# A first attention pair multiplied in plain fp32 instead of split products, and the order of work around it

## The chip, the cores and the metric

The kernel runs on one core of a Trainium2 chip. The metric is the device time of one execution in microseconds (us); the median of several executions is compared. The engines that matter are TensorE (PE, matrix products), VectorE (DVE), ScalarE (ACT), GpSimd (POOL) and SyncE (SP, whose queue issues the transfers).

## What is computed

One layer of a streaming encoder for 512 prompt tokens and 32 sample tokens, T = 544 tokens together, model width 2048. The input x is normalised, multiplied by one wide weight `w_in`, and the result goes to three groups of heads: eight retention heads, four spatial-gating groups, four heads of cross-attention to a memory of 256 tokens. The gated outputs are multiplied by `w_out` and added to x. All data are float32. The part that matters here:

```python
h = rmsnorm(x, g_norm)
proj = h @ w_in                            # 2048 -> 6656 columns
kv = rmsnorm(mem, g_mem) @ w_mem_kv        # keys and values of the memory
mk, mv = jnp.split(kv, 2, axis=-1)
...
sc = jnp.einsum('blhd,bmhd->bhlm', aq, mem_k) * (XA_HEAD_DIM ** -0.5)
p = jax.nn.softmax(sc, axis=-1)
ao = jnp.einsum('blhm,bmhd->blhd', p, mem_v) * silu(ag)
...
out = x + jnp.concatenate([ro, go, ao], axis=-1) @ w_out
```

## The kernel before

**Products in split form.** A float32 operand is split into a rounded high part (`copy`, ACT, line 87) and the rest as low part (`tt` with subtract, DVE, line 90); each product of a block is three matmuls: high x high, high x low, low x high (`multiply`, line 222). Plain float32 matmuls are used for small things only, such as scores (`sc`), transposes (`pT_ps`) and `ao`; in the profile each of these shows as two records.

**Pairs and blocks.** The columns of `w_in` are handled in pairs of 128 columns, called xa0 to xa3 (query and gate of an attention head), then qk and vg for the retention heads, gv and gg, and eight output pairs o0 to o7. In a pair the activations, laid out by feature, are cut in a 2 x 2 grid: two halves of the features (the outer index of `xk`) and two halves of the tokens (272 each). The blocks of x are called h11 and h21 (first feature half, first and second tokens), h12 and h22 (second feature half). Their split forms live in `A["11"]`, `A["21"]`, `A["12"]`, `A["22"]`.

**Seven products instead of eight.** All pairs but the first ones (xa0, o0) use seven block products on sums of blocks (`project`, line 238). For these the kernel makes S1 = h21 + h22, S2 = S1 - h11, S3 = h11 - h21 and S4 = h12 - S2 and splits each. Likewise sums of weight blocks are made (`sources`, line 173: t2, t1, t3, t4). The first pair xa0 uses the plain eight block products (`plain`, line 324), while the sums are made in `between` on the side.

**Weights ahead.** `begin` (line 198) loads a pair's two weight halves, forms the next block's weight sum and copies its high part; `ahead` (line 209) takes the low part of the oldest begun block and begins the next. `product` calls `ahead` and then multiplies. High and low weight parts have three buffers each, raw weight halves three ("raw").

**The start.** In the order written: the keys of the memory (`kps`, steps `key_unit`), the values (`value_unit` splits a weight chunk, `value` multiplies it into `vps`), and meanwhile the row sums for the two norms: `square_mem` and `halve` give rm for the memory, `square_x` (ACT, with a running sum) gives r for x. `token_factors` takes the power -0.5 on POOL, `diagonals` and `to_all_partitions` spread the factors over the partitions through PE; the results are `rm_bc` and `r_bc`. `scale_x` multiplies x by the gain and r (DVE, line 93), `split_x` and `block` split it. Then come xa0, xa1 (with the first head of `attend`) and so on. `attend` is a generator; `project` takes one step of it after each product: sigmoid part of the gate, scores and softmax, empty steps, transposes, output.

**Order.** `put` (line 82) keeps an instruction in program order on its engine as long as `fixed[0]` is true; it becomes false at the end of xa0. After that the framework orders the instructions itself. Transfers are issued on SP in the order of the loads: memory and key weights, tokens (`xt`, x by tokens for the row sums), value weights (`wv`), x by features (`x`, four quarters of 1088 KB), weights of xa0 (`wxa`).

Of the kernel before, what the change touches and what calls it, by code (L numbers as in the profile page):

```python
# [14 lines left out]
P = 128  # L15
# [8 lines left out]
XH = 4  # L24
# [52 lines left out]
def step_kernel(ctx: ExitStack, tc: tile.TileContext, a, o):  # L77
# [88 lines left out]
    def load_half(i, half):  # L166
        if i < len(ORDER):
            w = W.setdefault(ORDER[i], {})
            if half not in w:
                w[half] = raw_weight(f"w{ORDER[i]}_{half}")  # L170
                nc.sync.dma_start(out=w[half].rearrange("p k b c -> p (k b c)"), in_=a["w"][i, half])
# [21 lines left out]
    FOUR = {"xa0": ("11", "12", "21", "22"), "o0": ("11", "12", "21", "22"),  # L193
# [15 lines left out]
    def ahead(more=True):  # L209

        if done[0] < len(units):
            if done[0] == len(begun):
                begin()
            name, key = units[done[0]]
            src, u = begun[done[0]]
            tt(u[1], src, u[0].bitcast(F32), ALU.subtract)
            W[name][key] = u
            done[0] += 1
            if more:
                begin()  # L220
# [60 lines left out]
    def silu2(x, th):  # L281

        nc.scalar.activation(out=th, in_=x, func=AF.Tanh, scale=0.5)
        stt(x, th, 1.0, x, ALU.add, ALU.mult)
# [53 lines left out]
    with tc.tile_pool(name="mkv", bufs=1, reuse_waits="tile") as mkv, ExitStack() as ctx_x:  # L338
# [3 lines left out]
        with tc.tile_pool(name="pa", bufs=1, reuse_waits="tile") as pa:  # L342
# [31 lines left out]
            def halve(x, k):  # L374
                while k > 1:
                    k //= 2
                    tt(x[:, 0:k], x[:, 0:k], x[:, k:2 * k], ALU.add)
                return x[:, 0]
# [45 lines left out]
            load_tokens(3)  # L424
            load_x(0, 4)
            wv.append(load_kv("wv", 2))
# [11 lines left out]
            def square_mem(u):  # L438
                i, ks = u // 4, slice(u % 4 * 2, u % 4 * 2 + 2)
                put(nc.scalar.activation(out=mem[i][:, ks], in_=mem[i][:, ks], func=AF.Square))  # L440

            def key_unit(u):
                i, k0 = u // 4, u % 4 * 2
                if u < 8:
                    w, src = unit(f"k{u}", [P, 2, 512]), wk[u // 2][:, u % 2 * 2:u % 2 * 2 + 2]
                    if u:
                        copy(w[0], src)
                    for k in (k0, k0 + 1):
                        copy(mm[i][0][:, k], mem[i][:, k], scale=gm[:, KS * i + k:KS * i + k + 1])
                    if not u:  # L450
                        copy(w[0], src)
                    tt(w[1], src, w[0].bitcast(F32), ALU.subtract)
                    for k in (k0, k0 + 1):
                        stt(mm[i][1][:, k], mem[i][:, k], gm[:, KS * i + k:KS * i + k + 1], mm[i][0][:, k].bitcast(F32),
                            ALU.mult, ALU.subtract)
                    ku[u] = w
                if u:
                    square_mem(u - 1)
# [9 lines left out]
            for u in range(8):  # L468
                key_unit(u + 1)
                if u == 4:  # L470
                    part0 = halve(mem[0], KS)
                elif u == 6:
                    value_unit(0)
                    square_x(0)
                elif u == 7:
                    value_unit(1)
                    part1 = halve(mem[1], KS)
                    square_x(1)
                for k in range(2 * u, 2 * u + 2):
# [8 lines left out]
            def value(v):  # L488
                for k in range(2 * v, 2 * v + 2):
# [17 lines left out]
            value(0)  # L507
            ps = small("rm_ps")
# [3 lines left out]
            square_x(4)  # L512
            value_unit(3)
            square_x(2)
            value(1)
            d = diagonals(rm, P, 2, pa, "rm_d")
            value_unit(4)
            square_x(3)
            value(2)
            to_all_partitions(ps, d)  # L520
            value_unit(5)
            copy(rm_bc, ps[:, 0:MEM])
            r = token_factors(ssx[:, 0:5], "r")
            value(3)
            for h in range(XH):
                tt(mkT_p[:, h], kps[h][:, 0:MEM], rm_bc, ALU.mult)
            d = diagonals(r, P, 5, pa, "r_d")
            value_unit(6)
            value(4)
            ps = small("r_ps")  # L530
            to_all_partitions(ps, d)
            copy(r_bc, ps[:, 0:T])
            value_unit(7)
            scale_x(0, 0, 4)
            value(5)
            split_x(0, 0, 4)
            ahead()
            scale_x(0, 4, 8)
            value(6)
            split_x(0, 4, 8)  # L540
            ahead(False)
            value(7)
            block("21", xk[0][:, 1])
            for m in range(2):
                copy(mv_p[:, m], vps[:, m * 512:(m + 1) * 512], scale=rm[:, m:m + 1])


            first = const.tile([P, 2, T], F32, tag="cs", name="Xxa0")
            pair = first[:, 0, :], first[:, 1, :]
            h11, h21, h12, h22 = xk[0][:, 0], xk[0][:, 1], xk[1][:, 0], xk[1][:, 1]  # L550

            def between(j):
                if j == 0:
                    scale_x(1, 0, 4)
                    split_x(1, 0, 4)
                    load_half(1, 0)
                elif j == 1:
                    scale_x(1, 4, 8)
                    split_x(1, 4, 8)
                    nc.sync.dma_start(out=o["cache_k"], in_=mkT_p)  # L560
                elif j == 2:
                    block("22", h22)
                elif j == 3:

                    tt(h22, h21, h22, ALU.add)
                elif j == 5:
                    tt(h21, h11, h21, ALU.subtract)
                    tt(h11, h22, h11, ALU.subtract)
                    block("S2", h11)
                elif j == 7:  # L570
                    block("S1", h22)
                    load_half(1, 1)
                    nc.sync.dma_start(out=o["cache_v"].rearrange("(m p) c -> p m c", p=P), in_=mv_p)
                    put(nc.vector.tensor_scalar(out=gret, in0=gret, scalar1=0.5, scalar2=None, op0=ALU.mult))
                    fixed[0] = False
# [14 lines left out]
        with tc.tile_pool(name="px", bufs=1, reuse_waits="tile") as px:  # L590
            def attend(h, aq, sg):
# [7 lines left out]
                for (t0, t1) in ((0, 4), (4, 5)):  # L599
                    n = tokens(t0)  # L600
                    ps = small(f"sc{h}_{t0}")
                    for t in range(t0, t1):
                        matmul(ps[0:n, (t - t0) * MEM:(t - t0 + 1) * MEM],
                                         lhsT=aq[:, t * P:t * P + n], rhs=mkT_p[:, h] if t < 4 else mkT_s, start=True, stop=True)
                    nc.vector.tensor_reduce(
                        out=st[0:n, 0, t0:t1],
                        in_=ps[0:n, 0:(t1 - t0) * MEM].rearrange("p (t m) -> p t m", m=MEM),
                        axis=AX.X, op=ALU.max, negate=True)
                    nc.vector.tensor_scalar(out=st[0:n, 0, t0:t1], in0=st[0:n, 0, t0:t1], scalar1=DH ** -0.5,  # L609
                                            scalar2=None, op0=ALU.mult)  # L610
                    for t in range(t0, t1):
                        nc.scalar.activation(out=pr[0:n, t, :], in_=ps[0:n, (t - t0) * MEM:(t - t0 + 1) * MEM],  # L612
                                             func=AF.Exp, bias=st[0:n, 0, t:t + 1], scale=DH ** -0.5,
                                             accum_out=st[0:n, 1, t:t + 1])
                    nc.vector.reciprocal(out=st[0:n, 2, t0:t1], in_=st[0:n, 1, t0:t1])
                    nc.vector.tensor_scalar(out=st[0:n, 2, t0:t1], in0=st[0:n, 2, t0:t1], scalar1=0.5, scalar2=None,
                                            op0=ALU.mult)
                    for t in range(t0, t1):
                        copy(pr[0:n, t, :], pr[0:n, t, :], scale=st[0:n, 2, t:t + 1])
                yield  # L620
# [5 lines left out]
                for m in range(2):  # L626
                    ps = small(f"pT_ps{h}_{m}")
                    for t in range(5):
                        n = tokens(t)
                        nc.tensor.transpose(ps[:, t * P:t * P + n], pr[0:n, t, m * P:(m + 1) * P], ident[0:n, 0:n])  # L630
# [493 lines left out]
```

## Time and profile before

| | |
|---|---|
| median of 3 runs | 919.37 us (919.02 to 919.79) |
| the profiled execution, its time | 917.82 us |
| its span, first to last instruction | 916.0 us |
| mean granted TensorE clock | 0.983 |
| PE busy | 883.2 us (96%) |
| DVE busy | 712.8 us (78%) |
| ACT busy | 440.5 us (48%) |
| PE busy from 60 to 80, 80 to 100 and 100 to 120 us | 16.7, 16.5 and 14.9 of 20 us |
| granted clock in the same three stretches | 0.91, 0.91, 0.91 |

The span is a little shorter than the time, because the time also holds what lies around the first and the last instruction. The busy share is an average over the whole run; what a change in one stage is worth is read from that stage: which engine waits there, and for whom. A row of the timeline has the start and the length in us, the engine, the line, the operation with output and inputs, the shape, the count, and, in brackets, the idle time of the engine before it and what ended that. In a row of the waits stand the total time, the number of times and the longest. Matrix products are pipelined, so the distance of two starts, not the length of one, gives the rate.

### The profile page before, as it was taken

The page shows a single profiled execution, that of the slowest core. Times are in us where ns is not written, and L with a number is a line of the kernel's source. Part 1 is how long each engine was busy: PE and PEld are TensorE (multiplying, and loading weights), DVE is VectorE, ACT ScalarE, POOL GpSimd, SP SyncE. Part 2 cuts the span into 40 slices and gives each one's busy share as a digit, 9 for nine tenths or more (in the row PEclk, how much of TensorE's full clock was granted, in tenths as well). Part 3 has the DMA queues.
Part 4 walks back from the last instruction along what each step waited for, and adds up shares of the span by engine and source line. Part 5 has one row for each costly group of instructions (what it writes and reads, how often), then busy time and mean ns, then how long its engine had stood idle before and what let it go on. Part 6 is the DMA issues. An engine that isn't in the chain of part 4 may idle for free.

```text
span 916.0 us, 16090 instructions
## 1 busy us (share of the span) xinstructions
PE 883.2 (96%) x6716; PEld 853.6 (93%) x6716; DVE 712.8 (78%) x1010; ACT 440.5 (48%) x656; POOL 17.3 (2%) x21
## 2 busy tenths in 40 slices
PE   8978799999999999999999999999999999999994
PEld 7868699989999999999999999999999999999993
DVE  5677996558687786969686968778998997877775
ACT  6843565555444444435344444433544845554440
POOL 0000000000000000000000000000100000000000
PEclk8998999999999999999999999999999999999997
DMA  9973043222213222223232221327645965233204
GB/s 359 378 280 122 0 141 114 101 83 95 95 66 99 107 92 101 105 101 106 101 104 66 94 100 62 118 99 265 218 160 184 357 240 198 93 99 120 105 1 195
DMA packets 36776, 126.51 MB, mean 138 GB/s; under 512 B 3584, under 2 KB 19072, under 8 KB 26592
## 3 DMA queue, kind: packets, MB, share of 16 engines
q1 hardware_dynamic: 36128, 124.39, 38.2%
q10 hardware_dynamic: 576, 1.11, 0.4%
q8 instruction: 52, 0.85, 0.4%
q14 instruction: 20, 0.16, 0.1%
HBM read 110.51 MB, written 14.97 MB: 137 GB/s over the span
## 4 chain that ended last, share of the span: by engine, by line
PE 82%; DVE 7%; DMA 5%; issue 3%; ACT 2%; SPq 1%; POOL 0%; POOLq 0%; DVEq 0%; ACTq 0%
DMA wv<-in_wv 4%; PE o0p L96 3%; PE xa2y L96 1%; PE gg1y L96 1%; PE vg6y L96 1%; PE vg7y L96 1%; PE vg3y L96 1%; PE vg2y L96 1%; PE qk2y L96 1%; PE gv0y L96 1%; PE qk7y L96 1%; PE qk6y L96 1%; PE qk3y L96 1%; PE qk1y L96 1%; PE qk5y L96 1%
## 5 line engine op out<-in xcount | busy, mean ns | idle before, releaser
L87 ACT ACTIVATE h_qk<-wqk 128x1024 fp32r<-128x1024 f32 x24 | 25.4, 1058 | 54.1 <-PE qk0y L96 3.7
L87 ACT ACTIVATE h_vg<-wvg 128x1024 fp32r<-128x1024 f32 x24 | 25.3, 1054 | 48.1 <-PE qk1z L96 4.4
L90 DVE TENSOR_TENSOR l_qk<-wqk,h_qk 128x1024 fp32r<-128x1024 f32 x24 | 29.3, 1223 | 23.0 <-ACT h_qk L87 23.0
L87 ACT ACTIVATE h_o<-wo 128x1024 fp32r<-128x1024 f32 x25 | 26.4, 1058 | 29.0 <-PE o3y L96 2.5
L90 DVE TENSOR_TENSOR l_o<-wo,h_o 128x1024 fp32r<-128x1024 f32 x25 | 30.6, 1222 | 6.2 <-ACT h_o L87 6.2
L90 DVE TENSOR_TENSOR l_vg<-wvg,h_vg 128x1024 fp32r<-128x1024 f32 x24 | 29.2, 1216 | 3.6 <-ACT h_vg L87 3.6
L87 ACT ACTIVATE h_xa<-wxa 128x1024 fp32r<-128x1024 f32 x13 | 13.6, 1051 | 19.7 <-PE xa0p L96 7.6
L90 DVE TENSOR_TENSOR l_xa<-wxa,h_xa 128x1024 fp32r<-128x1024 f32 x13 | 15.9, 1220 | 7.0 <-ACT h_xa L87 7.0
L87 ACT ACTIVATE zT<-zT,gall 128x272 f32<-128x272 f32 x32 | 15.8, 516 | 8.9 <-DVE last L90 8.4
L137 POOL TENSOR_TENSOR stats<-stats,mhalf 128x5 f32<-128x5 f32 x8 | 9.4, 1170 | 548.8 <-DVE stats L750 548.8
L90 DVE TENSOR_TENSOR l_v<-wv,h_v 128x1024 fp32r<-128x1024 f32 x8 | 9.8, 1224 | 11.5 <-ACT h_v L87 11.5
L87 ACT ACTIVATE h_gg<-wgg 128x1024 fp32r<-128x1024 f32 x12 | 12.6, 1056 | 12.8 <-PE gg2y L96 3.7
L90 DVE TENSOR_TENSOR l_k<-wk,h_k 128x1024 fp32r<-128x1024 f32 x8 | 9.8, 1223 | 10.2 <-ACT h_k L87 10.2
L90 DVE TENSOR_TENSOR l_gg<-wgg,h_gg 128x1024 fp32r<-128x1024 f32 x12 | 14.6, 1217 | 2.0 <-ACT h_gg L87 2.0
L739 PE MATMUL po<-vN,sT 128*128 128x128 f32 (+1 forms) x80 | 14.3, 276 | 0.0
L90 DVE TENSOR_TENSOR cats<-cats 128x272 f32<-128x272 f32 x28 | 11.9, 433 | 2.9 <-DMA cats<-cat 2.6
L759 DVE TENSOR_SCALAR on<-po,stats 128x128 f32<-128x128 f32 (+1 forms) x40 | 13.3, 400 | 0.0
L87 ACT ACTIVATE h_gv<-wgv 128x1024 fp32r<-128x1024 f32 x6 | 6.4, 1059 | 14.3 <-PE gv0z L96 4.4
L612 ACT ACTIVATE pr<-sc,st 128x256 f32<-128x256 f32 (+1 forms) x20 | 9.0, 469 | 8.7 <-DVE st L609 8.7
L742 PE MATMUL po<-S,Xqk 128*128 128x128 f32 (+1 forms) x64 | 12.5, 277 | 0.0
L96 PE MATMUL k<-mm0h,h_k 128*128 128x256 f32 x32 | 10.2, 318 | 2.3 <-ACT h_k L87 2.3
L957 ACT ACTIVATE sq<-zT 128x272 f32<-128x272 f32 x26 | 10.3, 417 | 3.7 <-DVE zT L90 3.7
(1913 smaller groups left out, 3946.1 us busy)
## 6 DMA issues: line engine op xcount, KB each, us to landing
wqk<-in_w SPq DMA_DIRECT2D x16, 1024.0 KB, 4.8
wvg<-in_w SPq DMA_DIRECT2D x16, 1024.0 KB, 4.7
wo<-in_w SPq DMA_DIRECT2D x16, 1024.0 KB, 4.9
wxa<-in_w SPq DMA_DIRECT2D x8, 1024.0 KB, 5.7
wgg<-in_w SPq DMA_DIRECT2D x8, 1024.0 KB, 5.8
x<-in_xH SPq DMA_DIRECT2D x4, 1088.0 KB, 14.2
xt<-in_x SPq DMA_DIRECT2D x4, 1024.0 KB, 16.5
wv<-in_wv SPq DMA_DIRECT2D x4, 1024.0 KB, 17.2
```

The lines of the kernel that those rows point to most:

```text
L87: put(nc.scalar.activation(out=out, in_=in_, func=AF.Copy, scale=scale))
L90: put(nc.vector.tensor_tensor(out=out, in0=in0, in1=in1, op=op))
L96: put(nc.tensor.matmul(out, lhsT=lhsT, rhs=rhs, start=start, stop=stop, **more))
L137: nc.gpsimd.tensor_tensor(out=out, in0=in_, in1=mhalf[0:n, 0:1].to_broadcast([n, in_.shape[1]]), op=ALU.pow)
L612: nc.scalar.activation(out=pr[0:n, t, :], in_=ps[0:n, (t - t0) * MEM:(t - t0 + 1) * MEM], func=AF.Exp, bias=st[0:n, 0, t:t + 1], scale=DH ...
L739: nc.tensor.matmul(po[0:n, t * P:(t + 1) * P], lhsT=sT[0:n, t * P:t * P + n], rhs=v[0:n, t, :], start=True, stop=(t == 0))
L742: nc.tensor.matmul(po[0:n, t * P:(t + 1) * P], lhsT=q[:, t * P:t * P + n], rhs=S[:, t - 1 if t < 4 else 4, :], start=False, stop=True)
L759: nc.vector.tensor_scalar(out=on[0:n, t, :], in0=po[0:n, t * P:(t + 1) * P], scalar1=s_[0:n, t, 0:1], scalar2=s_[0:n, t, 4:5], op0=ALU.sub ...
L957: nc.scalar.activation(out=s, in_=z, func=AF.Square)
```

## The change

- xa0 is no longer split. Its weights and x stay in float32, and the eight block products are single float32 matmuls (`first_products`: 8 per block and feature half, 64 in all). `plain` is not used for xa0; its four weight units and the split block `A["21"]` are gone. The first weight half of xa0 is loaded into a tile of its own (tag "S3h") instead of a "raw" buffer.
- While these run, `A["12"]`, `A["22"]`, S1, S2 and xa1's first weight units are made. The sums are made in other places in memory: h11 becomes S3, h21 becomes S1, h22 becomes S2, h12 becomes S4.
- The squares of x come ahead of the squares of the memory's second half on ACT, and ahead of or between the first value steps; the memory's squares are done in four instructions of double size. r is computed after value step 4's weights, rm only between the first products. The third chunk of value weights is loaded ahead of the first quarter of x.
- The keys are copied out of PSUM unscaled by ACT and multiplied by rm later, in place, by DVE. The last addition of `halve` goes to a separate tile.
- `silu2`, the softmax of `attend` and the transposes are under `put`, and `fixed[0]` becomes false only after xa1. The remaining sums (S3, S4) come before the first attention head's steps and not beside them; `attend` has one empty step fewer; pairs no longer drain it.

The core of the diff:

```diff
@@ load_half
+                if i + half == 0:
+                    w[half] = ap.tile([P, KS, 2, P], F32, tag="S3h", name="wxa0_0")
+                else:
+                    w[half] = raw_weight(f"w{ORDER[i]}_{half}")
@@ units, ahead
-    FOUR = {"xa0": ("11", "12", "21", "22"), "o0": ("11", "12", "21", "22"),
+    FOUR = {"xa0": (), "o0": ("11", "12", "21", "22"),
...
-    def ahead(more=True):
+    def ahead():
...
-            if more:
-                begin()
+            begin()
@@ silu2
-        nc.scalar.activation(out=th, in_=x, func=AF.Tanh, scale=0.5)
+        put(nc.scalar.activation(out=th, in_=x, func=AF.Tanh, scale=0.5))
@@ halve
-                while k > 1:
+                while k > 2:
                     k //= 2
                     tt(x[:, 0:k], x[:, 0:k], x[:, k:2 * k], ALU.add)
-                return x[:, 0]
+                s = part("sqm")[:, 0:MEM]
+                tt(s, x[:, 0], x[:, 1], ALU.add)
+                return s
@@ loads
             load_tokens(3)
+            wv.append(load_kv("wv", 2))
             load_x(0, 4)
-            wv.append(load_kv("wv", 2))
@@ key_unit and the key steps
-                if u:
-                    square_mem(u - 1)
+                if u in (2, 4):
+                    square_mem(u - 2, 2)
...
                 elif u == 6:
+                    square_x(0)
                     value_unit(0)
-                    square_x(0)
+                    square_x(1)
                 elif u == 7:
                     value_unit(1)
-                    part1 = halve(mem[1], KS)
-                    square_x(1)
+                    square_x(4)
@@ value steps (new order)
+            square_x(2)
+            value_unit(3)
+            value(1)
+            square_x(3)
+            value_unit(4)
+            r = token_factors(ssx[:, 0:5], "r")
+            value(2)
+            square_mem(4, 2)
+            d = diagonals(r, P, 5, pa, "r_d")
+            value_unit(5)
+            value(3)
+            value(4, 0)
+            ps = small("r_ps")
+            to_all_partitions(ps, d)
+            copy(r_bc, ps[:, 0:T])
+            value(4, 1)
+            square_mem(6, 2)
+            scale_x(0, 0, 4)
+            value_unit(6)
+            for h in range(XH):
+                copy(mkT_p[:, h], kps[h][:, 0:MEM])
+            value(5)
+            value_unit(7)
+            scale_x(0, 4, 8)
+            value(6)
+            split_x(0, 0, 4)
+            split_x(0, 4, 8)
+            value(7)
@@ the first pair
+            (h11, h21), (h12, h22) = ((x[:, 0], x[:, 1]) for x in xk)
+            def first_products(i, c, g):
+                if i == 0:
+                    fps[c, g] = acc("YX"[c], f"xa0p{c}{g}")
+                for k in range(KS):
+                    matmul(fps[c, g][:, 0:TH], lhsT=W["xa0"][i][:, k, c, :], rhs=xk[i][:, g, k],
+                           start=i + k == 0, stop=i * k == KS - 1)
+                if i:
+                    copy(pair[c][:, g * TH:(g + 1) * TH], fps[c, g][:, 0:TH])
+            load_half(1, 0)
+            load_half(1, 1)
+            first_products(0, 0, 1)
+            scale_x(1, 0, 4)
+            scale_x(1, 4, 8)
+            first_products(0, 1, 1)
+            block("22", h22)
+            part1 = halve(mem[1], KS)
+            first_products(0, 0, 0)
+            split_x(1, 0, 4)
+            split_x(1, 4, 8)
+            ahead()
+            first_products(0, 1, 0)
+            tt(h11, h11, h21, ALU.subtract)
             ps = small("rm_ps")
             token_sums(ps, 512, part0, mem_tiles, True, False)
             token_sums(ps, 512, part1, mem_tiles, False, True)
             rm = token_factors(ps[:, 512:514], "rm")
+            tt(h21, h21, h22, ALU.add)
             d = diagonals(rm, P, 2, pa, "rm_d")
+            ahead()
+            block("S1", h21)
+            first_products(1, 0, 1)
             for m in range(2):
                 copy(mv_p[:, m], vps[:, m * 512:(m + 1) * 512], scale=rm[:, m:m + 1])
-            plain("xa0", lambda c, g, ps: copy(pair[c][:, g * TH:(g + 1) * TH], ps[:, 0:TH]), between)
+            first_products(1, 1, 1)
+            to_all_partitions(ps, d)
+            copy(rm_bc, ps[:, 0:MEM])
+            tt(h22, h22, h11, ALU.subtract)
+            for h in range(XH):
+                tt(mkT_p[:, h], mkT_p[:, h], rm_bc, ALU.mult)
+            block("S2", h22)
+            first_products(1, 0, 0)
+            nc.sync.dma_start(out=o["cache_k"], in_=mkT_p)
+            nc.sync.dma_start(out=o["cache_v"].rearrange("(m p) c -> p m c", p=P), in_=mv_p)
+            first_products(1, 1, 0)
             def last_sums():
-                block("S3", h21)
+                block("S3", h11)
                 yield
-                tt(h12, h12, h11, ALU.subtract)
+                tt(h12, h12, h22, ALU.subtract)
                 yield
                 block("S4", h12)
+                put(nc.vector.tensor_scalar(out=gret, in0=gret, scalar1=0.5, scalar2=None, op0=ALU.mult))
                 yield
@@ the heads (attend: softmax and transposes under put, three empty yields become two)
+            other = sums_left
             for h in range(XH):
-                other = attend(h, *pair)
-                if h == 0:
-                    other = together(sums_left, other)
+                other = chain(other, attend(h, *pair))
                 if h + 1 < XH:
-                    pair = project(f"xa{h + 1}", lambda name: px.tile([P, T], F32, tag="X", name=f"X{name}", bufs=3), other)
+                    pair = project(f"xa{h + 1}", lambda name: px.tile([P, T], F32, tag="X", name=f"X{name}", bufs=3), other, False)
+                    fixed[0] = False
```

More of the change, by code (lines that the diff above doesn't have):

```diff
@@ L169, in load_half @@
             if half not in w:
-                w[half] = raw_weight(f"w{ORDER[i]}_{half}")
+                if i + half == 0:
+                    w[half] = ap.tile([P, KS, 2, P], F32, tag="S3h", name="wxa0_0")
+                else:
+                    w[half] = raw_weight(f"w{ORDER[i]}_{half}")
                 nc.sync.dma_start(out=w[half].rearrange("p k b c -> p (k b c)"), in_=a["w"][i, half])
@@ L436, in step_kernel, with square_mem @@
             ku = {}
-            def square_mem(u):
-                i, ks = u // 4, slice(u % 4 * 2, u % 4 * 2 + 2)
+            def square_mem(u, n):
+                i, ks = u // 4, slice(u % 4 * 2, u % 4 * 2 + 2 * n)
                 put(nc.scalar.activation(out=mem[i][:, ks], in_=mem[i][:, ks], func=AF.Square))
@@ L486, in step_kernel, with value @@
             vps = small("vps")
-            def value(v):
-                for k in range(2 * v, 2 * v + 2):
+            def value(v, part=None):
+                for k in range(2 * v, 2 * v + 2) if part is None else (2 * v + part,):
                     for m in range(2):
@@ L507, in step_kernel @@
             value(0)
+            square_x(2)
[26 more added lines that the diff above has]
+            value(7)
+            first = const.tile([P, 2, T], F32, tag="cs", name="Xxa0")
+            pair = first[:, 0, :], first[:, 1, :]
+            (h11, h21), (h12, h22) = ((x[:, 0], x[:, 1]) for x in xk)
+            fps = {}
+            def first_products(i, c, g):
[20 more added lines that the diff above has]
+            tt(h11, h11, h21, ALU.subtract)
             ps = small("rm_ps")
@@ L511, in step_kernel @@
             rm = token_factors(ps[:, 512:514], "rm")
[L512 to L515, printed above, removed]
+            tt(h21, h21, h22, ALU.add)
             d = diagonals(rm, P, 2, pa, "rm_d")
[L517 to L536, printed above, removed]
-            ahead()
[L538 to L543, printed above, removed]
+            ahead()
@@ L544, in step_kernel @@
+            block("S1", h21)
+            first_products(1, 0, 1)
             for m in range(2):
                 copy(mv_p[:, m], vps[:, m * 512:(m + 1) * 512], scale=rm[:, m:m + 1])
[L548 to L575, printed above, removed]
@@ L604, in attend @@
                                          lhsT=aq[:, t * P:t * P + n], rhs=mkT_p[:, h] if t < 4 else mkT_s, start=True, stop=True)
-                    nc.vector.tensor_reduce(
+                    put(nc.vector.tensor_reduce(
                         out=st[0:n, 0, t0:t1],
                         in_=ps[0:n, 0:(t1 - t0) * MEM].rearrange("p (t m) -> p t m", m=MEM),
-                        axis=AX.X, op=ALU.max, negate=True)
-                    nc.vector.tensor_scalar(out=st[0:n, 0, t0:t1], in0=st[0:n, 0, t0:t1], scalar1=DH ** -0.5,
-                                            scalar2=None, op0=ALU.mult)
+                        axis=AX.X, op=ALU.max, negate=True))
+                    put(nc.vector.tensor_scalar(out=st[0:n, 0, t0:t1], in0=st[0:n, 0, t0:t1], scalar1=DH ** -0.5,
+                                            scalar2=None, op0=ALU.mult))
                     for t in range(t0, t1):
-                        nc.scalar.activation(out=pr[0:n, t, :], in_=ps[0:n, (t - t0) * MEM:(t - t0 + 1) * MEM],
+                        put(nc.scalar.activation(out=pr[0:n, t, :], in_=ps[0:n, (t - t0) * MEM:(t - t0 + 1) * MEM],
                                              func=AF.Exp, bias=st[0:n, 0, t:t + 1], scale=DH ** -0.5,
[L614 to L617, printed above, removed]
+                                             accum_out=st[0:n, 1, t:t + 1]))
+                    put(nc.vector.reciprocal(out=st[0:n, 2, t0:t1], in_=st[0:n, 1, t0:t1]))
+                    put(nc.vector.tensor_scalar(out=st[0:n, 2, t0:t1], in0=st[0:n, 2, t0:t1], scalar1=0.5, scalar2=None,
+                                                op0=ALU.mult))
                     for t in range(t0, t1):
                         copy(pr[0:n, t, :], pr[0:n, t, :], scale=st[0:n, 2, t:t + 1])
-                yield
                 yield
@@ L629, in attend @@
                         n = tokens(t)
-                        nc.tensor.transpose(ps[:, t * P:t * P + n], pr[0:n, t, m * P:(m + 1) * P], ident[0:n, 0:n])
+                        put(nc.tensor.transpose(ps[:, t * P:t * P + n], pr[0:n, t, m * P:(m + 1) * P], ident[0:n, 0:n]))
                     pT.append(px.tile([P, T], F32, tag=("pT", "th")[m], name=f"pT{h}{m}"))
```

## The prediction

> **What bounds the kernel now.** I read the page first. TensorE (PE) is busy almost throughout, so time can only come from stretches where it waits, runs at half rate, or does work that can go. Then the busy time by stretch (columns: PE, weight load, VectorE, ScalarE, GpSimd busy with counts; granted clock; DMA share; GB/s).
>
> ```profile
> PE 883.2 (96%) x6716; PEld 853.6 (93%) x6716; DVE 712.8 (78%) x1010; ACT 440.5 (48%) x656; POOL 17.3 (2%) x21
> ...
> 33.50:62.60 29.10, 26.38 (x112) 20.97 (x111) 18.46 (x25) 18.17 (x22) 1.88 (x2) 0.94 1.01 393
> 62.60:98.00 35.40, 28.60 (x193) 27.50 (x192) 29.11 (x28) 14.21 (x17) 0.00 (x0) 0.90 0.25 81
> 98.00:132.50 34.50, 29.37 (x200) 26.03 (x199) 33.51 (x39) 21.89 (x39) 0.00 (x0) 0.95 0.22 77
> ```
>
> The stretches are the value projection, pair xa0, pair xa1. In all three PE is short of full and the clock below 1; in xa1 VectorE (DVE) is busy 33.5 of 34.5 us. The changed code lies exactly here. The next fences are the waits of PE between 33 and 133 us (total, times, longest) and PE's timeline (start, length, what, idle before).
>
> ```profile
> PE xa1y L96 <- ACT h_xa1t L87: 3.6, 1, 3.6
> PE xa0p L96 <- ACT A11h L87: 2.4, 1, 2.4
> PE xa0p L96 <- ACT A12h L87: 2.3, 1, 2.3
> PE r_ps L96 <- DVE r_d L90: 1.8, 1, 1.8
> ```
>
> ```profile
> 62.62 0.29 PE L96 MATMUL xa0p<-A11h,h_xa 128*128 128x272 f32 x1
> ...
> 66.74 0.39 PE L96 MATMUL xa0p<-A11h,h_xa 128*128 128x272 f32 x1 [2.41 <-ACT A11h L87]
> ...
> 69.56 0.43 PE L96 MATMUL xa0p<-A11h,l_xa 128*128 128x272 f32 x1
> ...
> 98.02 0.29 PE L96 MATMUL xa1y<-A11h,h_xa 128*128 128x272 f32 x1
> ```
>
> xa0 is 192 matmuls and takes 62.6 to 98.0, 35.4 us. The chain of the undisturbed pair xa2 gives the full rate: 24 matmuls of 272 columns in 3.03 us, 0.126 each, so 24.2 us would do. The other 11 us are waits for the split (rounded high part, then low part) of x, and half-rate stretches after them (0.43 us rows).
>
> ```profile
> 132.50 3.03 PE xa2y L96 x24
> ...
> 138.55 2.28 PE sc L96 x10
> ...
> 147.07 1.37 PE pT_ps L630 x10
> ...
> 154.68 2.08 PE ao L96 x8
> ```
>
> xa1 takes 34.4 us to 132.5 where its seven products and one head of attention need 7 x 3.03 + 2.28 + 1.37 + 2.08 = 26.9.
>
> **The change, part by part.** Durations of ScalarE (ACT) and VectorE, and the arrival of transfers (issue, then us to landing):
>
> ```profile
> 26.50 0.89 ACT L87 ACTIVATE mm1h<-meml,gall 128x256 fp32r<-128x256 f32 x2
> ...
> 30.54 1.90 ACT L397 ACTIVATE xt<-xt 128x2048 f32<-128x2048 f32 x1
> ...
> 36.36 1.06 ACT L87 ACTIVATE h_v<-wv 128x1024 fp32r<-128x1024 f32 x1 [0.47 <-DMA wv<-in_wv]
> ...
> 44.10 1.06 ACT L87 ACTIVATE h_v<-wv 128x1024 fp32r<-128x1024 f32 x1 [1.76 <-DMA wv<-in_wv]
> ...
> 53.54 0.62 ACT L87 ACTIVATE r_bc<-r_ps 128x544 f32<-128x544 f32 x1 [3.19 <-PE r_ps L96]
> ...
> 83.45 1.11 ACT L87 ACTIVATE A12h<-x 128x1088 fp32r<-128x1088 f32 x1 [4.14 <-DVE x L93]
> 85.42 2.09 ACT L87 ACTIVATE A22h<-x 128x1088 fp32r<-128x1088 f32 x2
> ```
>
> ```profile
> 35.17 2.41 DVE L90 TENSOR_TENSOR meml<-meml 128x1024 f32<-128x1024 f32 x3
> ...
> 49.18 0.16 DVE L297 TENSOR_SCALAR r<-ssx 128x5 f32<-128x5 f32 x1
> ...
> 50.63 0.82 DVE L90 TENSOR_TENSOR r_d<-ct,r 128x640 f32<-128x640 f32 x1
> ...
> 55.14 1.22 DVE L90 TENSOR_TENSOR l_v<-wv,h_v 128x1024 fp32r<-128x1024 f32 x1 [2.54 <-ACT h_v L87]
> 56.28 2.86 DVE L93 SCALAR_TENSOR_TENSOR x<-x,gall,r_bc 128x544 f32<-128x544 f32 x4
> ...
> 86.94 2.49 DVE L90 TENSOR_TENSOR A22l<-x,A22h 128x1088 fp32r<-128x1088 f32 x2
> 89.46 2.42 DVE L90 TENSOR_TENSOR x<-x,x 128x2176 f32<-128x2176 f32 x1
> ```
>
> ```profile
> 23.04 0.33 SPq L387 DMA_DIRECT2D xt<-in_x  x1
> 25.37 0.64 SPq L354 DMA_DIRECT2D x<-in_xH  x1
> 49.68 0.55 SPq L354 DMA_DIRECT2D x<-in_xH  x1
> 87.09 0.33 SPq L171 DMA_DIRECT2D wxa<-in_w  x1
> ```
>
> ```profile
> xt<-in_x SPq DMA_DIRECT2D x1, 1024.0 KB, 15.8
> ...
> x<-in_xH SPq DMA_DIRECT2D x1, 1088.0 KB, 16.1
> ...
> x<-in_xH SPq DMA_DIRECT2D x1, 1088.0 KB, 9.8
> ...
> wxa<-in_w SPq DMA_DIRECT2D x1, 1024.0 KB, 4.6
> ```
>
> I carry each engine's queue in the order written, on the time axis of the profiled run; back to back, an instruction starts some 0.08 us before the one ahead has ended.
>
> *Squares of x first, wv2 ahead of x.* ACT is free at 27.4. Now: x0's square to 29.4, h_v0, x1, h_v1, the two short ones, h_v2 (waits for its weights at 36.3, as before), x2, h_v3, x3 42.1 (tokens 3 landed at 38.8). The third value weights landed at 44.0, right behind the first quarter of x at 25.4 + 16.1 = 41.5; DMA is full (share 1.01), so a swap exchanges landings: weights 41.4, x 44.0, needed only at 48.7. h_v4 runs 42.1, l_v4 ends 44.3, then r, GpSimd's power and r_d follow at the old distance (49.18 to 50.63): r_d 45.7, its PE sums 46.5, r_bc ends 48.7 instead of 54.2. That is 5.4 us earlier. The merged squares of the memory (two of 1.0 us for four of 0.6) go into ACT's gaps after h_v4 and r_bc: nothing.
>
> *Values, then xa0.* Twelve matmuls of 0.229 us per value step are 21.9 us, r's sums 1.1, waits for r_d and l_v6 0.7 each: from 33.5 to 58.2, where it was 62.6. x0 is scaled by 56.7 (l_v5, four scalings, l_v6, l_v7, four scalings), its weights, in a tile freed by x0's square at 29.4, need no weight buffer; no wait in front of the first fp32 product.
>
> *xa0 in fp32.* A row for 128x272 in fp32 without splitting isn't there. sc is: four matmuls of 256 columns plus one with 32 weight columns in 2.28, 0.456 each, so 0.484 for 272. 64 of them take 31.0 us against the 24.2 of 192 split ones: 6.8 us more PE work. Bounds: 0.38, the three split matmuls that each one replaces, and 0.97 at half rate; ao's 1088 columns in 2.08 would make it 0.52. I take 0.484, since sc too changes its weights with every matmul. At 0.38 nothing more is won, because DVE (below) then sets the end; at 0.52 everything after ends 2.3 later. With the memory's row sums and rm's broadcast (1.4), PE ends xa0 at 90.6. Gone are four weight splits (about 1.0 on ACT and 1.14 on DVE each) and the block A21 (2.1 and 2.5): 7 us of DVE work.
>
> *DVE beside it.* From 56.7: A11 2.4, x1 scaled to 64.8 (last quarter landed at 49.7 + 9.8 = 59.5), A22 to 67.2, part1 2.3, A12 to 71.9, xa1's first low part 73.1, h11 - h21 (waits for PE to 73.7) to 76.0, h21 + h22 78.5, rm's diagonal, low part 21, two weight sums to 82.2, S1 84.4 to 86.8 (it waits for ACT, which holds the copy of t2 first), S2's difference 89.2, four multiplications of the keys in place (0.3 each; the copies from PSUM are new on ACT, 4 x 0.29, in a gap), S2 to 92.8. PE and DVE thus end nearly together; moved output transfers of the keys sit in SP ahead of xa2's weights, which are needed 15 us later and took 4.6 to land.
>
> *What moves with it.* mv_p's two copies (0.6 each) wait for rm until 77.5 and stand on ACT behind S1's high parts, at 85.6; who waits for their PSUM buffer is the scores at 107.6. The four results of xa0 are copied (0.29 each) between 85.3 and 91.9; xa1's first accumulators are free by then, its third, at 99.7, as well. xa1's two weight loads move up in SP, behind the x quarters and into buffers that value steps 5 and 7 free at 48 and 54: landings about 62 and 65, one after the other, needed at 68. rm's chain comes 39 us later than before; only rm_bc, mkT_p and mv_p hang on it, needed at 107.6 at the earliest.
>
> *xa1 pinned.* Products 11 and 21 take PE from 90.6 to 96.7, t2 to 99.7, t1 (its low part ready 99.5) to 102.7. t3's low part waits behind the difference for S4: 104.5, a stall of 1.8. t3, scores (2.28), 22, t4: 115.7. Behind the scores DVE has reciprocals that wait for exponentials, and xa2's first low part behind these: 117.5, another 1.8. The transposes and ao of head 0 (3.45) now fall in xa2, so the place comparable with 132.3 is 117.5 + 3.45 = 121.0: 11.4 earlier.
>
> *The same carrying of the old order* gave r_bc at 53.2 (trace 53.54), the wait's end 66.4 (66.74), A12's second half 82.2 (83.45): up to 1.3 early over 35 us. I take 1.0 off: **gain 10.4**. The regions after xa2 keep work and order; free order there may add or take a few tenths. The halving of g_ret (0.1 on DVE), first needed in the retention heads, costs nothing; a head's attention has one empty step fewer, which only shifts it between products.
>
> *Half rate.* The row: after idle 2.4 and a further 0.9 within some 3.4 us, PE ran 0.226 instead of 0.126 per matmul for 3.3 us, which costs 1.6. My two stalls of 1.8 lie near that: 0 to 3.2 us; I take 0 and keep 3.2 for the range. The Trainium skill ("TensorE: Matmul & The Clock Gate", "What's actually happening") has the half clock come after at least one idle window of about 3.4 us. By that alone neither stall would cost: 907.4 for a profile; by the row at worst 910.6. The trace's stall was shorter than the page's window and still cost.
>
> **Sum.** The profiled run took 917.82 (span 916.0), 1.55 under the median of 919.37. 917.8 - 10.4 = 907.4; on the median 909.0.
>
> **The rivals.**
> 1. *The ping-pong of xa1 is slower than carried.* Three engines hand over at every product; VectorE is full there. For it: 33.5 of 34.5 us busy before. Against: DVE loses those 7 us, and the pinned order no longer puts a head's scores amid product t2, where PE now stood 3.6. Both half-rate stretches (3.2) and 2 us of late low parts leave a gain of 5: 914. Chance 0.18.
> 2. *xa1's second weights come as late as now.* Before they were issued at 87.1 and landed at 91.7. If SP holds them up again, t2's two weight sums wait to 92 instead of starting at 80, with S1, S2 and all of xa1 behind them in the queue: xa1 ends 13 later, no change: 918 to 920. Against: a weight buffer fewer is taken by xa0, so the third is free at 54, and the issue stands in the program ahead of the products. Chance 0.05.
> 3. *Slower: sustained fp32 doesn't keep the rate.* The longest full-rate fp32 run in the trace is 2.3 us; here are 31. At half rate, 0.97 each, xa0 ends at 121.5 instead of 90.6, xa1 at 146.6, comparable place 150: 17.7 later, 937. It decides from 0.65 us per matmul (10.4 / 64 = 0.16 over 0.484). Against: sc and ao, fp32 throughout, hold the rate amid full work. Chance 0.07.
>
> **How the numbers follow.** The forecast, gain 8 to 13, has 0.70. Its best case is all of 11.4 and one stall less: 906. Up to rival 1's 914 the range holds about 0.83. A change under 0.2% (1.8 us) can't be told from none. Faster 0.88 (forecast and rival 1), same 0.05 (rival 2), slower 0.07 (rival 3).
>
> **What would show it.** r_bc near 48 to 49 us instead of 53.5; first fp32 product near 58 to 59; 128 records of it with 0.48 between pairs and a clock of 1.00; xa0's end near 91; no wait for A11 or A12 on PE; in xa1 short stalls before t3 and at xa2's start; xa2 beginning near 118 with ao of head 0 inside. Wrong, if fp32 pairs are over 0.6 apart, if a weight transfer lands after 80, or if PE waits over 5 us in xa1.

## The result, and the profile after

The changed kernel takes 905.6 us (904.69 to 907.08), the one before 919.35; the ratio is 0.9852, 95% interval 0.9835 to 0.9869. That is 13.75 us less where 10.4 was forecast: 0.75 us more than the top of the forecast gain of 8 to 13, and 0.4 us under the 906 that the prediction called its best case. The sign and the mechanism held; the size did not.

The busy time by stretch, cut at the same places of the work as before (end of the values, the first pair, the second pair):

```profile
33.50:58.00 24.50, 23.25 (x99) 17.71 (x98) 16.14 (x19) 17.86 (x24) 1.18 (x1) 1.00 1.02 414
58.00:91.00 33.00, 33.00 (x157) 27.86 (x156) 29.99 (x32) 12.35 (x17) 2.87 (x1) 1.00 0.18 69
91.00:118.50 27.50, 24.79 (x182) 22.89 (x181) 23.30 (x30) 17.86 (x33) 0.00 (x0) 1.00 0.40 142
```

PE is full through the first pair and the granted clock is 1.00 in all three stretches (0.94, 0.90 and 0.95 before). What PE still waits for:

```profile
PE xa1y L96 <- DVE l_xa1t L90: 0.9, 1, 0.9
PE xa1z L96 <- DVE l_xa1t L90: 0.9, 1, 0.9
PE r_ps L96 <- DVE r_d L90: 0.9, 1, 0.9
PE xa1y L96 <- ACT xa1u L87: 0.5, 1, 0.5
```

The waits for A11 and A12 and the 3.6 us in product t2 are gone. PE's timeline, with fp32 products merged (x64 are 32 matmuls of two records):

```profile
58.41 14.83 PE L96 MATMUL xa0p<-x,wxa 128*128 128x272 f32 x64
73.08 0.95 PE L96 MATMUL rm_ps<-ones,sqm 128*128 128x1 f32 x8
73.89 7.58 PE L96 MATMUL xa0p<-x,wxa 128*128 128x272 f32 x32
...
81.73 7.50 PE L96 MATMUL xa0p<-x,wxa 128*128 128x272 f32 x32
88.87 0.50 PE L96 MATMUL xa1y<-A11h,h_xa 128*128 128x272 f32 x1
```

The first pair now runs from 58.4 to 88.9 (62.6 to 98.0 before): it starts 4.2 earlier and is 4.9 shorter. The chain that ended last shows the third and the fourth pair, and below it the fourth pair of the kernel before:

```profile
117.84 3.05 PE xa2y L96 x22
...
147.39 3.03 PE xa3y L96 x24
```

```profile
159.87 3.03 PE xa3y L96 x24
```

The fourth pair started at 159.87 and starts at 147.39, with the same heads behind it: 12.5 us gained, 4.2 + 4.9 as above and 3.3 in the second and third pair. After that nothing is won: the first output pair starts 12.3 earlier (725.8 to 713.5), the span is 12.0 shorter (916.0 to 904.0).

### The profile page after: what moved, and what is told of

Same layout as the page of the kernel before. It is cut to its first block, busy times and chain, and to the rows that moved or that the text cites. A ratio compares the mean times of both kernels' runs of the same rounds, so it can differ in the third digit from the quotient of the medians.

```text
span 904.0 us, 15945 instructions
## 1 busy us (share of the span) xinstructions
PE 881.7 (98%) x6652; PEld 848.2 (94%) x6652; DVE 705.7 (78%) x1004; ACT 434.6 (48%) x650; POOL 19.4 (2%) x21
## 4 chain that ended last, share of the span: by engine, by line
PE 79%; DVE 11%; DMA 3%; ACT 3%; issue 2%; POOL 1%; POOLq 0%; DVEq 0%; SPq 0%; ACTq 0%
PE o0p L96 3%; DMA wv<-in_wv 2%; PE o2y L96 1%; PE xa2y L96 1%; PE gg1y L96 1%; PE vg7y L96 1%; PE vg6y L96 1%; PE vg3y L96 1%; PE vg2y L96 1%; PE qk2y L96 1%; PE vg5y L96 1%; PE qk5y L96 1%; PE o6y L96 1%; PE o4y L96 1%; PE vg4y L96 1%
## 5 line engine op out<-in xcount | busy, mean ns | idle before, releaser
L87 ACT ACTIVATE h_vg<-wvg 128x1024 fp32r<-128x1024 f32 x24 | 25.3, 1055 | 48.1 <-PE qk1z L96 4.4
L90 DVE TENSOR_TENSOR l_o<-wo,h_o 128x1024 fp32r<-128x1024 f32 x25 | 30.5, 1221 | 6.2 <-ACT h_o L87 5.8
L96 PE MATMUL xa0p<-x,wxa 128*128 128x272 f32 x128 | 29.9, 393 | 0.0
L96 PEld LDWEIGHTS xa0p<-x,wxa 128*128 128x128 f32 x128 | 24.2, 190 | 4.9
L753 PE MATMUL po<-vN,sT 128*128 128x128 f32 (+1 forms) x80 | 14.2, 276 | 0.0
L90 DVE TENSOR_TENSOR l_xa<-wxa,h_xa 128x1024 fp32r<-128x1024 f32 x9 | 11.0, 1218 | 3.9 <-ACT h_xa L87 3.8
L87 ACT ACTIVATE h_gv<-wgv 128x1024 fp32r<-128x1024 f32 x6 | 6.4, 1059 | 14.3 <-PE gv0z L96 4.4
L756 PE MATMUL po<-S,Xqk 128*128 128x128 f32 (+1 forms) x64 | 12.5, 277 | 0.0
```

What stands on the lines that cost most here:

```text
L87: put(nc.scalar.activation(out=out, in_=in_, func=AF.Copy, scale=scale))
L90: put(nc.vector.tensor_tensor(out=out, in0=in0, in1=in1, op=op))
L96: put(nc.tensor.matmul(out, lhsT=lhsT, rhs=rhs, start=start, stop=stop, **more))
L753: nc.tensor.matmul(po[0:n, t * P:(t + 1) * P], lhsT=sT[0:n, t * P:t * P + n], rhs=v[0:n, t, :], start=True, stop=(t == 0))
L756: nc.tensor.matmul(po[0:n, t * P:(t + 1) * P], lhsT=q[:, t * P:t * P + n], rhs=S[:, t - 1 if t < 4 else 4, :], start=False, stop=True)
```

## The experiments

The kernel before, timed beside each run, had medians from 918.50 to 919.76. So two runs that were not timed together are best compared by their gains over it, which are given where they say something else than the plain times (13.75 is the changed kernel's in its first timing, 14.2 in its second); a difference of a few tenths is not shown either way.

**The spread of the kernel before.** No edit.

> The kernel before, unchanged. Its profiled run took 917.8 while its timed runs took 919.0 to 919.8. If the profiled run was just one of its quicker executions, more runs scatter from 917.8 to 920, with clocks around 0.98 that go with the times. If the profiled run differs from timed runs as a rule, every timed run stays at 919 or above and the profiled one at 917.8 again.

Ten runs gave 917.81 to 920.14, 24 of the same kernel beside them 917.58 to 919.96, median 919.08; the clocks, 0.980 to 0.985, don't follow the times. Of the first expectation the scatter holds, and only the clocks do not: 917.82, the run on which the sum was made, was among the quickest draws. Of the profiled run (918.26) the first rows of the first and of the second pair are, with the shortest, median and longest duration in ns and the first and last start in us:

```profile
L96 PE MATMUL xa0p<-A11h,h_xa x16: 287/292/428, 60.0 to 72.2; 128*128 128x272 f32 x16
L96 PE MATMUL xa1y<-A11h,h_xa x8: 287/290/292, 97.7 to 100.3; 128*128 128x272 f32 x8
```

Here the first pair starts at 60.0 instead of 62.6, with the same code, and yet the second starts at 97.7 (98.0) and the fourth, by the same rows, at 159.7 in both. So the division into 4.2 and 4.9 us above belongs to one execution; their sum is 8.8 by this one. The 0.5 us by which this run is longer come in behind the fourth pair: its first output pair starts at 726.3 instead of 725.8. The changed kernel again:

> The changed kernel, unchanged, on one chip with the run after it. Theory: the difference to the kernel before is 12 to 14 again, the profiled spans 916.0 and 904.0 being one draw each: 905 to 907. Rival: the 905.6 of the first timing was a quick draw, and 907 to 908 (a gain of 11 to 12, as the profiles have it) comes out.

905.52 (904.87 to 905.90), ratio 0.9847 (0.9834 to 0.9861), and a profiled run of 905.90. In the changed kernel the profiled runs (905.75, 905.90) lie at the median or above. So the profiles' difference of 12.1 understates the 13.7 to 14.2 of the medians.

**Early row factors alone**, on the kernel before:

```diff
             load_tokens(3)
+            wv.append(load_kv("wv", 2))
             load_x(0, 4)
-            wv.append(load_kv("wv", 2))
...
                 elif u == 6:
+                    square_x(0)
                     value_unit(0)
-                    square_x(0)
+                    square_x(1)
                 elif u == 7:
                     value_unit(1)
                     part1 = halve(mem[1], KS)
-                    square_x(1)
+                    square_x(4)
...
+            square_x(3)
             value_unit(4)
-            square_x(3)
+            r = token_factors(ssx[:, 0:5], "r")
...
```

> The kernel before with the row factors of x computed as early as in the changed one (third value weights loaded ahead of the first x quarter, squares of x ahead on ScalarE), the first pair still split, the memory's factors at their old place. Theory (three parts: an earlier start, no waits in the first pair, less VectorE work up to the second pair): r_bc near 48.5 us, the first pair starts 4 us earlier and keeps its waits for split x and its 35 us, gain 4, 915.3. Rival (the order is all that counts, fp32 only adds PE work): gain of 8 or more, 911 or less.

918.41, ratio 0.9989 (0.9978 to 0.9999): 0.7 of the expected 4 us, by the interval 0.1 to 2.0. Neither expectation was met. Two rows say where they went. VectorE, with r_bc ready at 50.5, stands until the low parts of the last value weights, which are written ahead of the scaling:

```profile
51.50 2.36 DVE L90 TENSOR_TENSOR l_v<-wv,h_v 128x1024 fp32r<-128x1024 f32 x2 [2.49 <-ACT h_v L87]
53.78 2.87 DVE L93 SCALAR_TENSOR_TENSOR x<-x,gall,r_bc 128x544 f32<-128x544 f32 x4
```

so x is scaled 2.5 us earlier and not 3.6. And the busy time from 58 to 98 us, first of the kernel before, then of this one, shows the same waits and a lower clock, 0.87 for 0.91:

```profile
58.00:98.00 40.00, 33.20 (x213) 31.25 (x212) 32.53 (x31) 17.22 (x20) 0.00 (x0) 0.91 0.32 107
```

```profile
58.00:98.00 40.00, 32.80 (x212) 31.16 (x211) 32.77 (x30) 17.46 (x20) 0.00 (x0) 0.87 0.28 96
```

The first pair starts 3.3 us earlier than in the first trace of the kernel before (59.3 for 62.6), the second 1.5 (96.5 for 98.0); the early start of a pair that then waits for splits is in part spent in these waits and at the lower clock.

**Early factors and a pinned second pair, products still split.** The run before, with `fixed[0] = False` moved behind the second pair and the attention steps written as in the changed kernel.

> As the run before, and the second pair and its attention steps in pinned order as in the changed kernel; only the fp32 products (and what they free) are missing. Theory: gain 5 to 7, 912.5 to 914.5, since the waits for A11 and A12 and seven us more of VectorE work remain. Rival (order alone): 908 or less, within 2.5 of the changed kernel.

921.49, ratio 1.0028 (1.0018 to 1.0038): slower than before. The step that failed is the theory's 5 to 7: the pin does not help a split first pair. PE's longest wait in its second pair is for a copy that ScalarE makes, in the pinned order, behind S1's high parts:

```profile
PE xa1y L96 <- ACT xa1u L87: 4.5, 2, 4.3
```

In the changed kernel the wait for this copy is 0.5. In the VectorE timeline S1 comes 20 us later than in the changed kernel:

```profile
105.10 2.49 DVE L90 TENSOR_TENSOR AS1l<-x,AS1h 128x1088 fp32r<-128x1088 f32 x2 [2.75 <-ACT AS1h L87]
```

The rival is refuted with more force: with the same pins, the changed kernel is 15.9 us faster (921.49 to 905.6). What separates the two are the fp32 products with the passes they free, the order in which the sums of x are made, the earlier loads of the second pair's weights, and the later place of the memory's factors; these were not separated.

**The order left free from the second pair on**, changed kernel:

```diff
+            fixed[0] = False
             sums_left = last_sums()
```

> The changed kernel with the order left free from the second pair on. Theory: the framework puts scores or sums where they make PE wait, as before, 1 to 3 us slower: 906.6 to 908.6. Rival: the pin does nothing, 905.6.

904.11 (901.95 to 904.31), ratio 0.9840 (0.9825 to 0.9854): every run is below the changed kernel's quickest of nine, 904.69. By plain times the pin costs 1.5; by the gains over the kernel before (14.4 against 13.75 and 14.2) only 0.2 to 0.6, and the intervals of the ratios overlap. So the theory had the sign wrong, and that the pin does nothing is not excluded. The trace is of the quickest of the four, 901.95 (the others took 903.9 to 904.3); in it the fourth pair starts at 143.7 for 147.2. Busy time from 88 to 118 us, first of the changed kernel, then with the free order:

```profile
88.00:118.00 30.00, 27.29 (x197) 25.19 (x196) 25.91 (x33) 18.50 (x33) 0.00 (x0) 1.00 0.43 150
```

```profile
88.00:118.00 30.00, 29.66 (x223) 28.35 (x222) 28.73 (x36) 18.85 (x37) 0.00 (x0) 1.00 0.44 150
```

VectorE works 2.8 us more in the stretch: the framework splits S3 between the sums of weights, and takes the third pair's low parts ahead of the reciprocals that wait for exponentials. With both kernels in free order the fp32 part, with all that comes with it, is worth 918.41 - 904.11 = 14.3, by gains 13.7.

**The third value weights late again**, changed kernel, the two loads swapped back:

> The changed kernel with the third value weights loaded behind the first x quarter again. Theory: they land 2.6 later, 44.3 instead of 41.7, r stands on VectorE behind their low part, so r_bc and all after it come 2.1 later: 907.7. Rival (a transfer that is hidden anyway): 905.6.

907.55, ratio 0.9874 (0.9859 to 0.9888), 2.0 slower, as the theory had it. ScalarE's r_bc starts 2.5 later than the changed kernel's 48.29:

```profile
50.77 0.63 ACT L87 ACTIVATE r_bc<-r_ps 128x544 f32<-128x544 f32 x1 [4.03 <-PE r_ps L96]
```

In the trace the pairs that follow start 2.4 to 2.5 later as well (the fourth at 149.7 for 147.2). Once no split stands between x and the products, a shift of the start goes through to the later pairs; it did not in the split kernel.

**Half the fp32 products, and a quarter more.**

```diff
-                for k in range(KS):
+                for k in range(i * KS // 2, KS // 2 + i * KS // 2):
```

> The changed kernel with only half of the first pair's products (four of eight k steps in each; the other half of that pair's sum is left out): 32 fp32 matmuls less, 14.7 us of PE work. Theory: VectorE's queue up to S2, S3 and the low parts sets the end of the second pair, so the third starts within 1 us of where it does now: 904.6 to 907.2, the upper end if PE's new waits bring half rate. Rival (PE sets the end): up to 14.7 faster, 891.

906.08, ratio 0.9865 (0.9851 to 0.9880): 14.7 us of PE work taken away and nothing won. The waits of PE and the busy time of the first pair:

```profile
PE rm_ps L96 <- DVE sqm L90: 3.5, 1, 3.5
PE rm_ps L96 <- DVE rm_d L90: 3.5, 1, 3.5
```

```profile
58.00:91.00 33.00, 25.05 (x115) 20.51 (x114) 29.99 (x32) 12.41 (x16) 2.87 (x1) 0.90 0.28 104
```

VectorE is busy 29.99 us as with all products, to the hundredth. Its queue also stands where it stood up to the third pair's first low part (116.48 for 116.58), and the third pair's first product starts at 115.7 for 115.8:

```profile
L96 PE MATMUL xa2y<-A11h,h_xa x8: 285/290/292, 115.7 to 120.2; 128*128 128x272 f32 x8
```

So VectorE's queue sets the end.

```diff
-                for k in range(KS):
+                for n in range(KS + 2):
+                    k = min(n, KS - 1)
```

> The changed kernel with 16 more fp32 matmuls in the first pair (the last k step three times instead of once; that pair's sum is not the reference's): 7.3 us more PE work. Theory: 2.7 us of it disappear in PE's present waits in the second pair, the rest is paid: 910.2. Rival A (PE has no slack): 912.9. Rival B (VectorE has all the say): 905.6.

912.47, ratio 0.9930 (0.9913 to 0.9947): 6.9 slower, by gains 7.7, close to rival A. The trace has the first pair at 59.8 to 97.6, 37.8 us for 30.5, and the third pair's first product at 123.4 instead of 115.8:

```profile
L96 PE MATMUL xa0p<-x,wxa x160: 390/392/476, 59.8 to 97.6; 128*128 128x272 f32 x160
```

Of the 7.6, 1.4 came in ahead of the first pair; the other 6.2 are most of the added 7.3. The 2.7 us of waits were no slack, because VectorE's sums overwrite h11, h21 and h22 in place and have to wait for the products that read them. For the first of these sums the trace shows the wait, which the changed kernel does not have there:

```profile
78.36 2.43 DVE L90 TENSOR_TENSOR x<-x 128x2176 f32<-128x2176 f32 x1 [3.47 <-PE xa0p L96]
```

So work added to PE moves VectorE's queue too. The two queues are tied: taking from PE wins nothing, adding to PE costs nearly all.

**The transposes of head 0**, the third pair pinned as well (`fixed[0] = h == 0`):

> The changed kernel with the third pair pinned as well, so that the transposes of head 0 stay behind the third pair's first product. Theory: PE waits for that product's low part (about 1.4 us at 116 to 118) with nothing to fill the time, 1.1 slower: 906.7. Rival: free order gains nothing there, 905.6.

907.13 (907.02 to 907.53), ratio 0.9879 (0.9864 to 0.9893), 1.5 slower, by gains 2.4. PE's longest wait is the one that the transposes fill in the changed kernel:

```profile
PE xa2y L96 <- DVE l_xa L90: 1.6, 1, 1.6
```

**S1 ahead of t2's weight step.**

```diff
-            ahead()
             block("S1", h21)
+            ahead()
```

> The changed kernel with the split of S1 written ahead of the weight step that forms t2, so that ScalarE makes S1's high parts at 78 instead of waiting to 83 for t2's sum. Theory: VectorE's 2.2 us of idle time before S1's low parts goes, PE's 2.3 us of waits in the second pair go with it: 903.4. Rival: the copy of t2 now comes later and its low part takes the place of the old wait: 905.6.

In the changed kernel ScalarE held the copy of t2 first, in front of S1's high parts:

```profile
82.91 1.06 ACT L87 ACTIVATE h_xa1t<-xa1T 128x1024 fp32r<-128x1024 f32 x1 [12.94 <-DVE xa1T L90]
```

```profile
85.00 2.49 DVE L90 TENSOR_TENSOR AS1l<-x,AS1h 128x1088 fp32r<-128x1088 f32 x2 [2.20 <-ACT AS1h L87]
```

Here S1's low parts start at 78.98 and the idle time is gone:

```profile
78.98 2.50 DVE L90 TENSOR_TENSOR AS1l<-x,AS1h 128x1088 fp32r<-128x1088 f32 x2 [0.21 <-ACT AS1h L87]
```

In the trace the fourth pair starts 1.5 us earlier (145.7 for 147.2), of which 0.5 was there at the first product (57.9 for 58.4). The time is 904.86 (903.96 to 906.24), ratio 0.9844 (0.9831 to 0.9858): 0.7 less than the changed kernel, inside the spread of either. The direction fits the theory; its 2.2 was too much, since a wait of 0.9 for rm_bc came in behind.

**The reciprocals one step later**, on top of S1 first.

> As the run before, and the reciprocals and scalings of the softmax put one step later, so that VectorE does not wait for exponentials (2.1 and 1.8 us) ahead of the third pair's first low part. Theory: 0.5 to 1.5 faster than the run before: 902 to 903. Rival: the transposes, which now come later, cost what is won: as the run before.

904.12 (903.34 to 905.23), ratio 0.9837 (0.9824 to 0.9851); 0.7 under the run before, again inside the spread. The third pair starts at 114.0 for 114.3, the fourth at 145.5 for 145.7, but so does the first, at 57.5 for 57.9. That the reciprocals were worth 0.5 or more isn't shown.

**S1 first and free order together.**

> The changed kernel with S1 split ahead of t2's weight step and with the order left free from the second pair on. Theory: the free order already fills VectorE's idle time before S1 with S3, so the two do not add up: within 1 us of the free order alone, 903 to 904.5. Rival: they add, 1.5 and 0.7: 903 or less.

903.73 (901.62 to 905.65), ratio 0.9830 (0.9813 to 0.9846), the fastest median of all, 0.4 from the free order alone by plain times and 1.6 by gains. That is inside the expected range, but with runs from 901.62 to 905.65 it isn't shown whether the two add up. The profiled run of this kernel was its slowest, and ScalarE's waits in it name a transfer:

```profile
ACT pr L628 <- DMA cat<-Xxa: 5.6, 1, 5.6
```

Its third pair takes 35.2 us where the free order alone took 31.0. In free order an attention buffer can come to wait for a landing, and the time scatters over 4 us; whether this wait is there in every slow run is open, as only one was looked at.

## Why the prediction was wrong

**What came out as worked out.** r_bc starts at 48.29 (carried: 48.1). The first fp32 product starts at 58.41 (58.2). S1's low parts start at 85.0 (84.4), S2's at 91.09 (90.4). The third pair's first low part, at the end of VectorE's queue, ends at 117.8 (117.5):

```profile
113.66 0.18 DVE L630 RECIPROCAL st<-st 128x4 f32<-128x4 f32 x1 [2.06 <-ACT pr L627]
...
116.32 0.15 DVE L630 RECIPROCAL st<-st 32x1 f32<-32x1 f32 x1 [1.80 <-ACT pr L627]
...
116.58 1.20 DVE L90 TENSOR_TENSOR l_xa<-wxa,h_xa 128x1024 fp32r<-128x1024 f32 x1
```

The waits before it, 2.06 and 1.80, are the reciprocals that were named. Half rate did not come: the clock is 1.00 throughout. But PE did not stand for 1.8 us at either place either; ahead of t3 it waited twice, 0.5 and 0.9, and at the third pair's start twice for 0.2.

**Term 1, the measured scale: 1.5 us.** The sum was made on one profiled run of 917.82, and both kernels were taken to sit 1.55 below their medians. The kernel before does, by 1.3 against 24 runs; the changed one sits at its median. The run to run spread of 2.4 us of the kernel before belonged in the range, and was not there. Between the two profiles the gain is 12.1, inside the forecast 8 to 13. Where in the execution a typical run of the kernel before loses the rest was not traced.

**Term 2, the discount: 1.0 us where 0.3 was due.** The hand carried queue of the old order ran up to 1.3 early, and 1.0 was taken off for that in the new order. In the new order 117.5 was carried and 117.8 measured, at the place that decides. Most of the old lateness had come in ahead of A12, where ScalarE stood 6.46 us in front of a weight copy (the profile names no releaser); the new first pair has no such copy, and it was charged all the same.

**Term 3, the stall at the third pair: 1.6 us.** The 1.8 us were counted as empty and the 3.45 us of transposes and `ao` of head 0 as added behind them. The free order put the transposes (1.37), behind two matmuls of the third pair (0.25), into the stall. Forcing them behind cost 1.5.

Together 10.4 + 1.0 - 0.3 + 1.6 = 12.7, against 12.5 measured at the fourth pair. Of these, 0.4 are lost further on, and term 1 makes 12.1 into 13.7. So the steps that failed are three sizes: a discount for a wait that the new order does not have, a stall counted as empty that the framework filled, and one quick run taken as the scale, without the spread in the range.

**Slips in the working that changed little.** The terms named for the values end at 57.9 and not at 58.2 (58.41 measured). The two idle times ahead of the half rate lie within 3.7 us, from 64.33 to 68.06, and the 3.3 us at 0.226 instead of 0.126 per matmul cost 1.5 and not 1.6. A second pair that ends 13 later would by the prediction's own 11.4 have been slower than before, not 918 to 920.

**A size that was off and didn't matter.** The fp32 matmul took (73.08 - 58.41) / 32 = 0.458, not 0.484, so PE ended the pair 1.7 earlier than carried. That won nothing, as the half products show: VectorE sets the end. This part of the prediction is shown; its counterpart, 2.3 later at 0.52, wasn't tested singly, but the added products cost most of their time.

**The rivals.** Slow sustained fp32: refuted, 29 us of it at 0.458 and a clock of 1.00. Late weights: refuted, the second pair's two loads landed at about 62 and 65, as carried, ScalarE copied them from 67.98 on, and no wait names them. A slower ping-pong in the second pair: no; its waits sum to 2.3 us.

**Where the reason was incomplete.** The prediction had r_bc 5.4 us earlier and carried all of that through; it never asked what each part would bring without the others. Early factors alone are worth some 0.7, and the pin gains nothing and may cost up to 1.5; nearly all of the gain needs the rewritten first pair, in which no split stands in front of PE. How much of the 14 to 16 us belongs to the work freed, how much to the order of the sums, the earlier weight loads and the later place of rm, wasn't separated. The 5.4 us themselves were in part a draw: r_bc started at 53.54 in the first trace of the kernel before and at 52.0 in the second, and that made no difference behind the first pair.

## What to carry to other kernels

Where a pipeline starts up, more work on the matrix engine can be cheaper than the vector work that prepares cheaper passes: 5 us more PE work (64 x 0.458 against 24.2) came with a gain of 14, because PE had been waiting for the splits that the cheaper passes need, and VectorE's queue sets the end of the stretch. Work out such a start by carrying every engine's queue from the rows, and do not subtract a flat allowance: look which wait caused the lateness of the old order and whether the new order still has it. Count a stall at a pair's end as free room for whatever the framework may still move, and take the scale from the median, with the spread in the range.

## What the runs showed of the hardware

A plain fp32 matmul of 272 columns takes 0.458 us in a long stream, 3.6 times the 0.126 of one matmul of a split product, not four times: a split one runs at 272 / 0.126 = 2.16 columns per ns, the fp32 one at 4 x 272 / 0.458 = 2.38 if it goes over the columns four times, which no run here shows. The Trainium skill ("TensorE: Matmul & The Clock Gate", "Back-to-back issue gap") gives N / 2.4 + 2.5 ns for what it calls the isolated gap of a warm matmul. An estimate by it is 115.8 ns for 272 columns, and 0.463 us for four of these; the fp32 stream lies 1% under that, while the split one, at 126 ns, lies 9% over 115.8.

With half the products PE stood twice for 3.5 us and the clock was 0.90 in that stretch. In the kernel before, idle times of 2.4 and 0.9 us within 3.7 were followed by 3.3 us at 0.226 per matmul, and the 1.8 us ahead of r's sums by matmuls of 512 columns at 0.43 instead of 0.23:

```profile
51.60 1.90 PE L96 MATMUL r_ps<-r_d,ones 128*128 128x512 f32 x4 [1.83 <-DVE r_d L90]
...
54.15 0.63 PE L96 MATMUL vps<-h_v,mm1l 128*128 128x512 f32 x1
54.58 0.63 PE L96 MATMUL vps<-h_v,mm1h 128*128 128x512 f32 x1
```

Waits of 0.9 us, as in the changed kernel, left the clock at 1.00, and so did the 1.6 us in the run with the pinned transposes, behind which the matmuls kept 0.126.
